# Second FFN of a diffusion layer: gated tiles turned by VectorE and DRAM, column blocks in pairs

## The chip, the core and the metric

The kernel runs on one core of one Trainium2 chip. The metric is the device time of one execution in microseconds; several executions are taken and their median is given. Everything is fp32, and the products that need fp32 accuracy are made from two halves: each operand is split into a rounded high part and the low rest, and three matmuls (high times high, low times high, high times low) stand for one product.

## The reference

The reference computes one layer of a diffusion backbone for 256 latent and 256 context tokens at width 2048: a half-step SwiGLU FFN, a mixing stage, a second half-step FFN for the latent tokens alone, and a final RMSNorm. The change lies in the second FFN, whose hidden width is 5632:

```python
def half_step_ffn(x, mod, i, g, w_up, w_down):
    h = adaln(x, g, mod, i)
    a, b = jnp.split(h @ w_up, 2, axis=-1)
    return x + 0.5 * mod[:, i + 2, None, :] * ((jax.nn.silu(a) * b) @ w_down)
```

## The kernel before

The hidden width of the second FFN is cut into eleven blocks of 512 columns (`FB` = 4 times 128), numbered 0 to 10. Block 0 is made in the order that the down projection needs. Blocks 1 to 9 (`QUADS`) go through `quad(n)`, which multiplies 2 x 2 quarters of the token matrix with quarters of the weights in seven products instead of eight: sums of token quarters (`n1`, `s4`, `s2`, `s3`) are made once, sums of weight quarters are made by loads that accumulate (`accum`, line 740, GpSimd's queue) into the tiles called `chain2` and `ra`, and two PSUM banks X and Y collect the products. Block 10 (`LAST`) goes through the plain `up`.

Each quad has seven products in order, each of two half-steps `q`: a11, a12, n1, s4, s2, s3, a22. Every half-step takes 128 x 2048 weights, which `split` (lines 128 and 129) turns into `hi` on ScalarE and `lo` on VectorE in two halves of 1024, and 12 matmuls. The `hi` and `lo` tiles have four buffers each, so the splits run at most two steps ahead of TensorE. A gated tile (128 tokens x 512 hidden columns) is silu(a) times b. Tile t = 0 of a block is finished by `c12`, after s2; tile t = 1 by `c21`, after a22.

The down projection needs the hidden columns on the partitions, so each gated tile has to be turned. `wait_turn(n, t, sa, sign)` puts the tile into the list `turn`; `turned()` (line 2044) is called after each step, and once `N_TURN` steps have passed and a slot of the three hidden blocks in flight (`N_HID`) is there, it makes four transposes on TensorE into a PSUM bank of the pool `tr` (line 2058), and splits the bank into `hid2h` on ScalarE (line 2061) and `hid2l` on VectorE (line 2063). `born` and `clock` count steps.

`down(n, n + 1)` is the down projection of two blocks: for each of four column blocks `cb` it takes two PSUM banks, multiplies block n and then block n + 1 into them, and adds the banks into `acc2`. Each of its steps is one load of weights (`load_split`, line 143, SyncE's queue, three `raw` buffers) and 24 matmuls.

`sequence()` weaves the two streams: "s" is a half-step of a quad, "u" a step of `up` or `down`. From the second quad on, a "u" stands after a12, n1, s2 and s3, so a quad is 14 half-steps and four steps. After the last step the rest of `turn` is emptied, and the down projection of blocks 8 and 9 and then that of block 10 follow. SyncE issues all loads of raw, the plain loads of `chain2` and `ra`, in one queue; a load that waits holds the ones behind it. The order of the instructions on an engine is made by a scheduler that goes by the order in the code and by when it takes an instruction's inputs to be ready.

The first FFN already turns the tiles of its blocks 1 to 10 in the way that the change brings to the second: `nc.vector.transpose` on VectorE (line 840), which turns each 32 x 32 square in its place, a store to DRAM (line 842), and four fetches for each quarter of a raw buffer that exchange the bands of 32 (line 711). There the blocks are fetched when their down projection begins.

Of the kernel before, what the change touches and what calls it, by code (L numbers as in the profile page):

```python
# [58 lines left out]
def tile_layer(ctx: ExitStack, tc: tile.TileContext, I: dict, out: bass.AP):  # L59
# [81 lines left out]
    def load_split(src, n=2048):  # L141
        raw = raw_tile(n)
        nc.sync.dma_start(raw, src)
        wt = split(raw, n)
        next(beside["load"], None)
        return wt
# [594 lines left out]
    with pool(name="f1u", bufs=1) as f1u:  # L741
# [91 lines left out]
        def turned():  # L833

            if not turn:
                return
            n, t, ca, spare = turn.pop(0)
            if (n, t) == (NB - 1, 3):
                spare = chp.tile([P, CB], F32, tag="stg", name="stg")
            pinned(nc.vector.transpose(spare, ca))  # L840
            s, tt = divmod(t, 2)
            nc.sync.dma_start(hidd[n][2 * tt + s], spare)
# [1088 lines left out]
    with f2x:  # L1931
        def hid_tiles():

            return [f2.tile([P, FB, T], F32R, tag=g, name=g, bufs=N_HID) for g in ("hid2h", "hid2l")]
# [106 lines left out]
        summed = set()  # L2041
        born, clock = {}, [0]

        def turned():

            if not turn:
                return
            n, t, sa, sign = turn[0]
            if clock[0] < born[n, t] + N_TURN:
                return  # L2050
            if n not in hids:
                if n - 1 not in hids or len(hids) - len(summed) >= N_HID:
                    return
                hids[n] = hid_tiles()
            turn.pop(0)
            tb = tbank()
            for j in range(FB):
                nc.tensor.transpose(tb[:, j * P : (j + 1) * P], sa[:, j * P : (j + 1) * P], ident)  # L2058
            t3 = tb.rearrange("p (j c) -> p j c", j=FB)
            hh, hl = (x[:, :, t * P : (t + 1) * P] for x in hids[n])  # L2060
            nc.scalar.activation(hh, t3, AF.Copy, scale=sign)
            if sign < 0:
                nc.vector.scalar_tensor_tensor(hl, t3, -1.0, hh.bitcast(F32), op0=ALU.mult, op1=ALU.subtract)
            else:
                nc.vector.tensor_tensor(hl, t3, hh.bitcast(F32), op=ALU.subtract)
            done.add((n, t))

        done = set()

        def wait_turn(n, t, sa, sign):  # L2070
            turn.append((n, t, sa, sign))
            born[n, t] = clock[0]
            turn.sort(key=lambda x: x[:2])

        def ca_tile():
            return f2b.tile([P, CB], F32, tag="ca", name="ca", bufs=3)

        def quad(n):

            add = lambda o, x, y: nc.vector.tensor_tensor(o, x, y, op=ALU.add)  # L2080
            mul = lambda o, x, y: nc.vector.tensor_tensor(o, x, y, op=ALU.mult)
            B, g = {}, {}

            def p1():
# [25 lines left out]
            def c21():  # L2110
                add(g["a"], B["Y"], g["a"])
                nc.scalar.activation(g["a"], g["a"], AF.Silu)
                mul(g["a"], g["a"], g["y"])
                wait_turn(n, 1, g["a"], -1.0)

            def chained(ab, c):
                return lambda q: accum(chain_[q], part(n, ab, c + q))
# [62 lines left out]
        def up(n):  # L2180

            sab = []
            for ab in range(2):
                bs = [bank() for _ in range(2)]
                for u in range(4):
                    wt = load_split(part(n, ab, u))
                    for j in range(4):
                        k = 4 * u + j
                        w = slice(j * CB, (j + 1) * CB)
                        for t in range(2):  # L2190
                            tt = slice(t * P, (t + 1) * P)
                            mm3(bs[t], h2hi[:, k, tt], h2lo[:, k, tt], *wt(w), k == 0, k == KT - 1)
                    if u == 3:
                        for t in range(2):
                            if ab:
                                nc.vector.tensor_tensor(sab[t], sab[t], bs[t], op=ALU.mult)
                                wait_turn(n, t, sab[t], 1.0)
# [14 lines left out]

        def down(*ns):

            for cb in range(NCB):
                c = slice(cb * CB, (cb + 1) * CB)
                bs = [bank() for _ in range(2)]
                for n in ns:
                    assert (n, 1) in done or not n
                    wt = load_split(I["w_dn2"][n, cb])  # L2220
                    for t in range(2):
                        block(bs[t], n, wt, t, n == ns[0], n == ns[-1])
                    if n == ns[-1]:
                        for t in range(2):
                            a = acc2[:, t, c]
                            if not ns[0]:
                                nc.scalar.activation(a, bs[t], AF.Copy)
                            else:
                                nc.vector.tensor_tensor(a, a, bs[t], op=ALU.add)
                            if n == LAST - 1:  # L2230
                                half_gated(a, a, late["g8"][:, c])
                                accum(a, x2d[t * P : (t + 1) * P, c])
                        if cb == NCB - 1:
                            summed.update(ns)
                    yield

        def units():
            yield from up(LAST)
# [37 lines left out]
        drain(down(LAST - 2, LAST - 1))  # L2276

        def last2():

# [69 lines left out]
def _laid_out(a):  # L2349
# [30 lines left out]
    for n in "12":  # L2380
        up, dn = a[f"w_ffn{n}_up"][0], a[f"w_ffn{n}_down"][0]
        nf = dn.shape[0] // P
        up = up.reshape(KT, P, 2, nf, P)

        rest = up[:, :, :, FB:].reshape(4, 4, P, 2, nf // FB - 1, CB)
        m[f"w_up{n}b"] = asc(rest.transpose(4, 3, 0, 2, 1, 5).reshape(nf // FB - 1, 2, 4, P, 2048))
        first = up[:, :, :, :FB].transpose(3, 2, 1, 0, 4).reshape(-1, 2, P, 2048)
        m[f"w_up{n}"] = asc(first[NPRE:])
        pre = first[:NPRE].reshape(2 * NPRE, P, KT, P)
        loads = []  # L2390
        for k0, k1 in BLOCKS if n == "1" else BLOCKS2:
# [3 lines left out]
        rows = dn.reshape(NF // FB, FB, P, NCB, CB).transpose(0, 3, 2, 1, 4).reshape(NF // FB, NCB, P, 2048)  # L2395
        if n == "1":
            turned = dn.reshape(NF // FB, 4, FB, 32, NCB, CB).transpose(0, 4, 1, 3, 2, 5).reshape(NF // FB, NCB, P, 2048)
            rows = np.concatenate([rows[:1], turned[1:]])
        m[f"w_dn{n}"] = asc(rows)
    w = a["w_in"][0]  # L2400

# [32 lines left out]
```

## Time and profile before

| What | Value |
| --- | --- |
| Median of 3 runs | 2591.18 us (2589.92 to 2593.5) |
| Profiled execution | 2588.91 us |
| its span | 2587.2 us |
| Granted TensorE clock, mean | 0.995 |
| Nine blocks of the second FFN | about 1950 to 2515 us of the span |

The profile is of one execution. Times in it are counted from the start of the span; what lies around the span is 1.7 us. An instruction of TensorE is shown with a modelled end, so the distance between two starts is what one takes when they follow each other closely. A wait is put down to what came last.

### The profile page before, as it was taken

What the parts mean: (1) busy time and instruction counts of PE and PEld (TensorE: products, weight loads), DVE (VectorE), ACT (ScalarE), POOL (GpSimd) and SP (SyncE); (2) the same over time, 40 slices, a digit from 0 to 9 for tenths busy, and PEclk for the clock granted to TensorE, in tenths of its full rate; (3) what the DMA queues carried; (4) which work ended last, traced back from release to release, by engine and by line L of the source; (5) the groups of instructions that cost most, each with busy time, mean ns of one, the idle gap of its engine ahead of it and who ended that gap; (6) DMA issues with size and microseconds to landing.
All of it is one profiled execution on the core that took longest, in us unless ns stands there. A gap on an engine that the chain in (4) does not pass through costs nothing. (4 is left out here: it accounts for less than half of the span.)

```text
span 2587.2 us, 33868 instructions
## 1 busy us (share of the span) xinstructions
PE 2555.3 (99%) x12486; PEld 2124.7 (82%) x12486; DVE 2206.6 (85%) x2924; ACT 1405.5 (54%) x1798; POOL 221.9 (9%) x271
## 2 busy tenths in 40 slices
PE   8999999999999999999999999999999999999998
PEld 5788888888887878888889889888898888888886
DVE  7789888888888788888887888898889888898987
ACT  5454444444444455444454347466486676667763
POOL 0000000100010100010110000120000000000001
PEclk8999999999999999999999999999999999999999
DMA  9989999999999999999987897776768999999985
GB/s 392 355 214 275 265 290 277 262 292 281 276 285 282 255 236 246 213 221 231 231 242 268 295 315 242 237 282 212 267 233 246 275 277 283 278 286 278 273 248 171
DMA packets 153478, 684.70 MB, mean 265 GB/s; under 512 B 22872, under 2 KB 43864, under 8 KB 92000
## 3 DMA queue, kind: packets, MB, share of 16 engines
q1 hardware_dynamic: 123936, 490.64, 51.7%
q0 software_dynamic: 29376, 191.90, 37.3%
q8 instruction: 98, 1.61, 0.2%
q14 instruction: 68, 0.56, 0.1%
HBM read 664.59 MB, written 17.89 MB: 264 GB/s over the span
## 5 line engine op out<-in xcount | busy, mean ns | idle before, releaser
L128 ACT ACTIVATE hi<-raw 128x1024 fp32r<-128x1024 f32 (+2 forms) x488 | 504.5, 1040 | 401.2 <-PE mm L152 298.7
L129 DVE TENSOR_TENSOR lo<-raw,hi 128x1024 fp32r<-128x1024 f32 (+2 forms) x476 | 567.2, 1204 | 105.7 <-ACT hi L128 87.4
L128 ACT ACTIVATE hi<-chain 128x1024 fp32r<-128x1024 f32 x352 | 370.1, 1059 | 352.6 <-PE mm L152 199.3
L129 DVE TENSOR_TENSOR lo<-chain,hi 128x1024 fp32r<-128x1024 f32 x352 | 425.2, 1219 | 92.5 <-ACT hi L128 81.2
L152 PE MATMUL mm<-hi,hhi 128*128 128x512 f32 (+3 forms) x1024 | 390.7, 382 | 0.0
L152 PE MATMUL mm<-lo,hhi 128*128 128x512 f32 (+3 forms) x1024 | 387.7, 379 | 1.9 <-DVE lo L129 1.8
L152 PE MATMUL mm<-hi,hlo 128*128 128x512 f32 (+3 forms) x1024 | 386.6, 378 | 0.0
L208 DVE SCALAR_TENSOR_TENSOR junk<-sraw,cBh 128x1024 fp8e5<-128x1024 f32 x192 | 234.3, 1220 | 40.5 <-DMA sraw<-in_w_mt 39.0
L152 PEld LDWEIGHTS mm<-lo,hhi 128*128 128x128 f32 x1024 | 192.8, 188 | 37.0 <-DVE lo L129 4.0
L152 PEld LDWEIGHTS mm<-hi,hlo 128*128 128x128 f32 x1024 | 193.0, 189 | 32.0
L152 PEld LDWEIGHTS mm<-hi,hhi 128*128 128x128 f32 x1024 | 192.9, 188 | 32.2 <-ACT hi L128 0.3
L129 DVE TENSOR_TENSOR lo<-ra,hi 128x1024 fp32r<-128x1024 f32 x104 | 126.2, 1222 | 25.6 <-ACT hi L128 21.7
L128 ACT ACTIVATE hi<-ra 128x1024 fp32r<-128x1024 f32 x104 | 110.1, 1062 | 64.0 <-PE mm L152 34.2
L152 PE MATMUL mm<-lo,hid2h 128*128 128x512 f32 x352 | 137.1, 389 | 0.0
L152 PE MATMUL mm<-hi,hid2h 128*128 128x512 f32 x352 | 137.1, 389 | 0.0
L152 PE MATMUL mm<-hi,hid2l 128*128 128x512 f32 x352 | 137.0, 389 | 0.0
L152 PE MATMUL mm<-hi,sumshl 128*128 128x512 f32 x400 | 123.2, 389 | 0.0
L208 DVE SCALAR_TENSOR_TENSOR sr<-sr,cBl 128x1024 f32<-128x1024 f32 x84 | 102.1, 1222 | 16.4 <-DMA sr<-in_w_mt 15.1
L740 POOL DMA_DIRECT2D chain<-in_w_up1b x60 | 53.1, 886 | 724.1 <-DVE lo L129 583.9
L152 PE MATMUL mm<-hi,sumshh 128*128 128x512 f32 x352 | 108.3, 389 | 0.0
L152 PE MATMUL mm<-hhi,hi 128*128 128x512 f32 (+1 forms) x288 | 101.4, 352 | 0.0
L152 PE MATMUL mm<-hhi,lo 128*128 128x512 f32 (+1 forms) x288 | 99.0, 344 | 0.0
(490 smaller groups left out, 5415.1 us busy)
## 6 DMA issues: line engine op xcount, KB each, us to landing
raw<-in_w_dn SPq DMA_DIRECT2D x70, 1024.0 KB, 10.0
chain<-in_w_up1b POOLq DMA_DIRECT2D x60, 1024.0 KB, 10.7
sraw<-in_w_mt SPq DMA_DIRECT2D x96, 512.0 KB, 8.4
sr<-in_w_mt SPq DMA_DIRECT2D x81, 512.0 KB, 5.7
raw<-in_w_up1b SPq DMA_DIRECT2D x40, 1024.0 KB, 9.1
mraw<-in_w_m SPq DMA_DIRECT2D x32, 1024.0 KB, 7.6
chain<-in_w_dn POOLq DMA_DIRECT2D x30, 1024.0 KB, 10.2
chain<-in_w_up2b POOLq DMA_DIRECT2D x28, 1024.0 KB, 11.4
```

Of the source, the lines that this page charges most:

```text
L128: scalar[0].activation(hi, src, AF.Copy)
L129: vector[0].tensor_tensor(lo, src, hi.bitcast(F32), op=ALU.subtract)
L152: tensor[0].matmul(out_ap, s, m, start=first and not n, stop=last and n == 2, skip_group_check=skip)
L208: ins = nc.vector.scalar_tensor_tensor(junk() if junk else raw, raw, 1.0, cB[s], op0=ALU.mult, op1=ALU.mult, accum_out=mT[:, i, s, kt, h : ...
L740: accum = lambda dst, src: nc.gpsimd.dma_start(dst, src, accum_op=ALU.add)
```

## The change

Tiles of blocks 1 to 9 are turned without TensorE. `c12` and `c21` multiply with a minus sign (`negative`) and hand a second tile, the one that held b, to `wait_turn` as `spare`. At the end of that step (`N_TURN` = 1, the count before was 2) `nc.vector.transpose` writes the tile into `spare`, turned in squares of 32. One step after that SyncE stores it to DRAM (`hid2d`); `N_STORE` = 3 steps after the turn, SyncE fetches it back into the first tile with four transfers, each of which puts one column band onto one band of 32 partitions in runs of 512 bytes; `N_MOVE` = 6 steps after the turn `halves` splits it into `hid2h` and `hid2l`, reading the four 32-wide runs of each group. The rows of the down weights of these blocks are laid out in the order that this gives. Block 10 still goes over TensorE, into a bank of the pool `mm`, which has six buffers; the pool `tr` is gone. The tiles `ca` have four buffers instead of three.

`down` takes two column blocks at a time: block n for both, then block n + 1 for both, in four banks. At the end its first two steps for blocks 8 and 9 run before the last gated tile is split.

```diff
-N_TURN = 2
+N_TURN = 1
+N_STORE = 3
+N_MOVE = 6
...
-        ps["mm"] = ctx.enter_context(pool(name="ps2", bufs=4, space=PSUM))
+        ps["mm"] = ctx.enter_context(pool(name="ps2", bufs=6, space=PSUM))
         psx = ctx.enter_context(pool(name="psx", bufs=1, space=PSUM))
-        ps["tr"] = ctx.enter_context(pool(name="pt2", bufs=2, space=PSUM))
...
+        hid2d = {n: dr.tile([2, P, CB], F32, name=f"hid2{n}") for n in QUADS}
+        moved = []
+        def halves(n, t, x, runs=False):
+            hh, hl = (y[:, :, t * P : (t + 1) * P] for y in hids[n])
+            if runs:
+                hh, hl = (y.rearrange("p j (a c) -> p a j c", c=32) for y in (hh, hl))
+            nc.scalar.activation(hh, x, AF.Copy)
+            nc.vector.tensor_tensor(hl, x, hh.bitcast(F32), op=ALU.subtract)
+            done.add((n, t))
...
-            for j in range(FB):
-                nc.tensor.transpose(tb[:, j * P : (j + 1) * P], sa[:, j * P : (j + 1) * P], ident)
-            t3 = tb.rearrange("p (j c) -> p j c", j=FB)
-            hh, hl = (x[:, :, t * P : (t + 1) * P] for x in hids[n])
-            nc.scalar.activation(hh, t3, AF.Copy, scale=sign)
-            if sign < 0:
-                nc.vector.scalar_tensor_tensor(hl, t3, -1.0, hh.bitcast(F32), op0=ALU.mult, op1=ALU.subtract)
...
+            if spare is not None:
+                turn.pop(0)
+                nc.vector.transpose(spare, sa)
+                moved.append((clock[0], n, t, sa, spare))
+            elif room(n):
+                turn.pop(0)
+                tb = bank()
+                for j in range(FB):
+                    nc.tensor.transpose(tb[:, j * P : (j + 1) * P], sa[:, j * P : (j + 1) * P], ident)
+                halves(n, t, tb.rearrange("p (j c) -> p j c", j=FB))
+        def stored(n, t, sa, spare):
+            nc.sync.dma_start(hid2d[n][t], spare)
+        def fetched(n, t, sa, spare):
+            rows = hid2d[n][t].rearrange("(a r) (b x) -> b r a x", a=4, b=4)
+            for b in range(4):
+                nc.sync.dma_start(sa[32 * b : 32 * b + 32].rearrange("r (a x) -> r a x", a=4), rows[b])
+        def arrived():
+            for then, *x in moved:
+                if clock[0] == then + 1:
+                    stored(*x)
+                elif clock[0] == then + N_STORE:
+                    fetched(*x)
+            if moved and clock[0] >= moved[0][0] + N_MOVE and room(moved[0][1]):
+                _, n, t, sa, _ = moved.pop(0)
+                halves(n, t, sa.rearrange("p (a j c) -> p a j c", a=4, j=FB), True)
...
-            return f2b.tile([P, CB], F32, tag="ca", name="ca", bufs=3)
+            return f2b.tile([P, CB], F32, tag="ca", name="ca", bufs=4)
...
-                mul(g["a"], g["a"], g["b"])
-                wait_turn(n, 0, g["a"], -1.0)
+                negative(g["a"], g["b"])
+                wait_turn(n, 0, g["a"], g["b"])
...
-            for cb in range(NCB):
-                c = slice(cb * CB, (cb + 1) * CB)
-                bs = [bank() for _ in range(2)]
+            for c0 in (0, 2):
+                bs = {}
                 for n in ns:
+                    for cb in (c0, c0 + 1):
...
             clock[0] += 1
+            arrived()
             turned()
...
-        while turn:
-            clock[0] += 1
-            turned()
-        before_final()
-        drain(down(LAST - 2, LAST - 1))
+        before_final()
+        final = down(LAST - 2, LAST - 1)
+        for gap in (1, N_STORE - 1):
+            clock[0] += gap
+            arrived()
+            next(final)
+        while moved:
+            clock[0] += N_MOVE
+            arrived()
+        while turn:
+            turned()
+        drain(final)
```

More of the change, by code (lines that the diff above doesn't have):

```diff
@@ L2047, in turned @@
                 return
-            n, t, sa, sign = turn[0]
+            n, t, sa, spare = turn[0]
             if clock[0] < born[n, t] + N_TURN:
                 return
[L2051 to L2056, printed above, removed]
-            for j in range(FB):
-                nc.tensor.transpose(tb[:, j * P : (j + 1) * P], sa[:, j * P : (j + 1) * P], ident)
@@ L2068, in tile_layer, with wait_turn @@
         done = set()
-        def wait_turn(n, t, sa, sign):
-            turn.append((n, t, sa, sign))
+        def wait_turn(n, t, sa, spare):
+            turn.append((n, t, sa, spare))
             born[n, t] = clock[0]
@@ L2112, in c21 @@
                 nc.scalar.activation(g["a"], g["a"], AF.Silu)
-                mul(g["a"], g["a"], g["y"])
-                wait_turn(n, 1, g["a"], -1.0)
+                negative(g["a"], g["y"])
+                wait_turn(n, 1, g["a"], g["y"])
             def chained(ab, c):
@@ L2213, in down @@
         def down(*ns):
-            for cb in range(NCB):
-                c = slice(cb * CB, (cb + 1) * CB)
-                bs = [bank() for _ in range(2)]
+            for c0 in (0, 2):
+                bs = {}
                 for n in ns:
[L2219 to L2223, printed above, removed]
-                        for t in range(2):
[L2225 to L2235, printed above, removed]
+                    for cb in (c0, c0 + 1):
+                        assert (n, 1) in done or not n
+                        c = slice(cb * CB, (cb + 1) * CB)
+                        if n == ns[0]:
+                            bs[cb] = [bank() for _ in range(2)]
+                        wt = load_split(I["w_dn2"][n, cb])
+                        for t in range(2):
+                            block(bs[cb][t], n, wt, t, n == ns[0], n == ns[-1])
+                        if n == ns[-1]:
+                            for t in range(2):
+                                a = acc2[:, t, c]
+                                if not ns[0]:
+                                    nc.scalar.activation(a, bs[cb][t], AF.Copy)
+                                else:
+                                    nc.vector.tensor_tensor(a, a, bs[cb][t], op=ALU.add)
+                                if n == LAST - 1:
+                                    half_gated(a, a, late["g8"][:, c])
+                                    accum(a, x2d[t * P : (t + 1) * P, c])
+                            if cb == NCB - 1:
+                                summed.update(ns)
+                        yield
         def units():
@@ L2395, in _laid_out @@
         rows = dn.reshape(NF // FB, FB, P, NCB, CB).transpose(0, 3, 2, 1, 4).reshape(NF // FB, NCB, P, 2048)
+        turned = dn.reshape(NF // FB, 4, FB, 32, NCB, CB).transpose(0, 4, 1, 3, 2, 5).reshape(NF // FB, NCB, P, 2048)
         if n == "1":
-            turned = dn.reshape(NF // FB, 4, FB, 32, NCB, CB).transpose(0, 4, 1, 3, 2, 5).reshape(NF // FB, NCB, P, 2048)
             rows = np.concatenate([rows[:1], turned[1:]])
+        else:
+            rows = np.concatenate([rows[:1], turned[1:-1], rows[-1:]])
         m[f"w_dn{n}"] = asc(rows)
```

13 lines of the change are left out of this document (8 added, 5 removed).

## The prediction

> **What bounds the kernel now.** I read the page's busy times first, then the table by stage for the stretch in which the nine blocks run, then TensorE's timeline at one of the groups of transposes that go.
>
> ```profile
> span 2587.2 us, 33868 instructions
> PE 2555.3 (99%) x12486; PEld 2124.7 (82%) x12486; DVE 2206.6 (85%) x2924; ACT 1405.5 (54%) x1798; POOL 221.9 (9%) x271
> ...
> core 0: us, PE busy (x) PEld busy (x) DVE busy (x) ACT busy (x) POOL busy (x), PEclk, DMA share, GB/s
> 2000.00:2500.00 500.00, 499.46 (x2232) 412.21 (x2231) 438.35 (x416) 347.15 (x367) 41.89 (x48) 1.00 0.94 275
> ```
>
> In these 500 us TensorE is busy for 499.46, at the full granted clock, so a stall of another engine costs nothing until TensorE waits for it, and an instruction taken from TensorE is time gained. A block of the nine is 14 half-steps of 12 matmuls, four steps of 24 and 8 transposes: 272 of the 2232 instructions, or 60.9 us. The same row gives a second number almost as full: the DMA engines are at 0.94.
>
> ```profile
> q0 software_dynamic: 7312, 53.35, 52.8%
> q1 hardware_dynamic: 11849, 86.19, 41.5%
> ...
> ACT hi L128 <- DMA chain<-in_w_up2b: 18.1, 7, 3.9
> ```
>
> These are the two queues over 1990 to 2500 us: the accumulating loads that GpSimd issues (q0) take the larger share, SyncE's plain loads (q1) the rest. The third line, of the waits, says that ScalarE already waits for an accumulated chain, up to 3.9 us, once in nearly every block.
>
> **What the change takes away.** 18 groups of four transposes on TensorE.
>
> ```profile
> 2000.12 0.39 PE L152 MATMUL mm<-lo,h2hi 128*128 128x512 f32 x1
> 2000.35 0.60 PE L2058 MATMUL tr<-ident,ca 128*128 128x128 f32 x4
> 2000.70 0.71 PE L152 MATMUL X<-hi,s3f 128*128 128x512 f32 x2
> 2001.26 0.40 PE L152 MATMUL X<-lo,s3f 128*128 128x512 f32 x1
> ...
> L2058 PE MATMUL tr<-ident,ca x72: 270/272/304, 2000.3 to 2514.6; 128*128 128x128 f32 x72
> ```
>
> The starts count, since durations overlap. A matmul's pitch is 2000.35 - 2000.12 = 0.23 us. From the first transpose to 2001.26 lie four transposes and two matmuls: 0.91 - 0.46 = 0.45 us for the group. 72 transposes are 18 groups: 8.1 us off TensorE, the whole of the gain, and a block falls from 60.9 to 60.0 us.
>
> **What it puts on VectorE and ScalarE.**
>
> ```profile
> L840 DVE STREAM_TRANSPOSE c<-ca x20: 691/704/711, 208.3 to 922.5; 128x512 f32<-128x512 f32 x20
> ...
> L2063 DVE SCALAR_TENSOR_TENSOR hid2l<-tr,hid2h x18: 683/684/694, 2002.6 to 2515.5; 128x512 fp32r<-128x512 f32 x18
> ...
> L2061 ACT ACTIVATE hid2h<-tr x20: 578/585/602, 2001.3 to 2515.4; 128x512 fp32r<-128x512 f32 x20
> ```
>
> The first FFN turns tiles of this shape on VectorE in 0.704 us (line 840): 18 x 0.704 = 12.7 us. VectorE is idle for 61.7 us of the 500 and takes them there; without that cover they would be 12.7 us. The sign moves from the low half (0.684 us) into the product, both 128x512, so neither side changes. The split into halves reads SBUF in place of PSUM; I keep 0.585 and 0.684 us. The pairs of column blocks in the down projection have the same matmuls and weights in another order, and the six banks hold what four and two held: nothing on the path while the next block's tiles are there, which the last tile below decides.
>
> **What it puts on the DMA rings.** 18 stores and 72 fetches. A store of 0.262 MB at q1's rate (86.19 MB in 41.5% of 510 us) is 0.64 us of all engines. The fetches move runs of 512 B. In the first FFN there is a stretch, 1004 to 1008 us, where nothing else moves:
>
> ```profile
> q1 hardware_dynamic: 1861, 0.93, 122.8%
> ```
>
> 0.93 MB in 4 us: 0.262 MB are 1.13 us. Two tiles per block add 3.5 us. The rings need 0.94 x 60.9 = 57.2 us per block now and 60.7 after, against 60.0 of TensorE. So the slack of the rings is gone. The bound of this is from 0 (the share was not all necessary time) to 0.7 us per block.
>
> **The wait that it adds.** Before, a tile went through PSUM in under 2 us. Now the split on ScalarE stands behind a store and a fetch that itself waits on SyncE for the store to land. Queued behind the split on ScalarE are the weight splits of the next steps, and TensorE waits for those; behind the fetch on SyncE are the next raw, ra and chain loads. The price is the round trip against the time to the split's place in ScalarE's order.
>
> ```profile
> 2185.44 0.68 DVE L2081 TENSOR_TENSOR ca<-ca 128x512 f32<-128x512 f32 x1
> 2202.55 3.49 DVE L129 TENSOR_TENSOR lo<-chain,hi 128x1024 fp32r<-128x1024 f32 x3
> 2208.82 0.69 DVE L2081 TENSOR_TENSOR ca<-ca,cy 128x512 f32<-128x512 f32 x1
> ...
> 2198.58 2.15 ACT L128 ACTIVATE hi<-ra 128x1024 fp32r<-128x1024 f32 x2 [2.22 <-DMA ra<-in_w_up2b]
> 2201.01 1.06 ACT L128 ACTIVATE hi<-chain 128x1024 fp32r<-128x1024 f32 x1 [0.29 <-PE Y L152]
> ...
> 2216.48 1.06 ACT L128 ACTIVATE hi<-chain 128x1024 fp32r<-128x1024 f32 x1 [0.30 <-PE Y L152]
> 2218.07 0.63 ACT L2090 ACTIVATE ca<-ca 128x512 f32<-128x512 f32 x1 [0.54 <-DVE ca L2080]
> 2222.41 2.01 ACT L128 ACTIVATE hi<-chain 128x1024 fp32r<-128x1024 f32 x2 [3.70 <-DMA chain<-in_w_up2b]
> ...
> 2205.07 0.39 PE L152 MATMUL X<-hi,h2hi 128*128 128x512 f32 x1
> ...
> 2227.17 0.50 PE L152 MATMUL Y<-lo,n1f 128*128 128x512 f32 x1 [0.53 <-DVE lo L129]
> ```
>
> Tile 0 of this block: product done at 2186.1, turned at 2186.8. Six steps later by the kernel's clock is after the last split of the block (hi<-ra, done 2200.7) and before that of the next block's first step (2201.01): 14.2 us from 2186.8. Tile 1: turned at 2210.2; six steps later is after the first half of n1's split (2216.48) and the silu (2218.07), before the second half at 2222.41: 12.2 us.
>
> ```profile
> L842 SPq DMA_DIRECT2D hid<-c x20: 326/327/1792, 209.1 to 923.2; - x20
> ...
> DMA to landing us min/median/max: 3.7/7.6/12.5
> ...
> L711 SPq DMA_DIRECT2D hidh<-hid x20: 325/480/704, 949.0 to 1229.8; - x20
> ...
> DMA to landing us min/median/max: 3.2/7.2/28.8
> ```
>
> Line 842 stores such tiles, line 711 fetches with the same exchange of bands; both stand in a stretch whose rings are as full. Ends: 3.7 + 3.2 and 12.5 + 28.8 us. I take the medians, as the rings here are no emptier, and three more issues before the last of four fetches, 3 x 0.48: 7.6 + 1.4 + 7.2 = 16.2 us, and 0.58 for the split's own activation.
>
> Tile 0: 16.8 - 14.2 = 2.6 us late on ScalarE. The low half of that next split ends by 2203.8 (the first of three from 2202.55) where TensorE wants it by about 2205.3: 1.5 us of cover, so 1.1 us of stall, 9 times: 9.9 us. Tile 1: 16.8 - 12.2 = 4.6 us, with no cover (TensorE waits there already, 0.53 us at 2227.17), 8 times: 36.8 us. Together 46.7 us. But a block that is 5 us longer leaves the rings 5 us more, and round trips shorten; between all of it and none I take half, 23.4 us.
>
> SyncE's held loads I cost at nothing:
>
> ```profile
> 2193.79 0.33 SPq L143 DMA_DIRECT2D raw<-in_w_dn  x1
> ...
> DMA to landing us min/median/max: 5.4/10.6/12.0
> ...
> 2212.46 1.05 ACT L128 ACTIVATE hi<-raw 128x1024 fp32r<-128x1024 f32 x1
> ```
>
> The raw block issued at 2193.79 lands by 2204.4 (median of line 143) and is split at 2212.46, three buffers later: 8.1 us of cover against a hold of at most a store's landing, 7.6. Without that cover it would be up to 7.6 us a block.
>
> The last tile 1:
>
> ```profile
> 2513.41 0.68 DVE L2081 TENSOR_TENSOR ca<-ca,cy 128x512 f32<-128x512 f32 x1
> ...
> 2510.62 0.19 PEld L152 LDWEIGHTS mm<-hi,hid2h 128*128 128x128 f32 x1
> ```
>
> Turned at 2514.8; with 8.3 to 16.2 us of round trip (minimum and median, with the issues) and 1.3 of halves its block could start between 2524.4 and 2532.3. TensorE has two steps of block 8 (48 matmuls, 10.9 us), 12 matmuls of tile 0 (2.7) and the group for the last block (0.9). Its weight load at 2510.62 opens the two steps, so it gets there at about 2525: 0 to 7 us; few loads are left, so I take 1.
>
> Sum: -8.1 + 23.4 + 1 = +16.3 us, on a profiled execution of 2588.91 us: 2605.2. That execution was 2.3 us under the median of 2591.18, so 2607.5 on the scale of the runs. What a measurement of this kernel can tell from no change is about 0.2%, 5.2 us.
>
> **The rivals.** *All hidden, faster.* If the two landings and the issues take under 12 us together, no split is late, and the 8.1 us stay: 2583 to 2586. For it: the minima add up to 8.3 us; and in the first FFN TensorE stays full with the same stores at a DMA share of 0.99:
>
> ```profile
> 600.00:680.00 80.00, 80.00 (x355) 66.07 (x354) 70.37 (x96) 36.97 (x42) 7.05 (x8) 1.00 0.99 279
> ```
>
> Against it: there the fetch comes tens of microseconds after the store, here after two steps. 0.28. The Trainium skill, "DMA: Bandwidth & Descriptors", section "Anatomy of one DMA", fits a transfer as 2.0 us plus bytes over 436 GB/s: an estimate of 2.6 us for a store, by which this rival would win. The median of 7.6 us says that a full ring is not that case.
>
> *The rings become the bound, no change.* No split is late, but the rings need 60.7 us a block where TensorE needs 60.0: nine blocks of 60.7 instead of 60.9 are 2 us less, and the last tile gives 1 to 4 back: 2588 to 2595. For it: the sum above. Against it: it needs every other wait hidden. 0.12.
>
> *The fetch starves, much slower.* Where q0 has a backlog, the rings alternate packet by packet, so a fetch of 32 small packets per engine waits for 32 large accumulating ones. The first FFN shows it, 885 to 901 us:
>
> ```profile
> q0 software_dynamic: 445, 3.25, 97.6%
> q1 hardware_dynamic: 445, 0.23, 6.9%
> ```
>
> One for one, and such a fetch landed after up to 28.8 us. Tile 1's fetch falls where q0 holds two accumulating loads. If all of it does, ScalarE waits 20 us more there, and even half of that in five of the blocks is 50 us: 2640 to 2680. Against it: the two loads are gone after some 14 us. 0.15. The Trainium skill (same page, "Queues, rings and completion order") has an engine drain a packet of about 9 to 17 descriptors before it turns to another ring; by that the fetch would pass in three or four turns and this rival would fall. The equal counts in the rows speak against that here.
>
> **How the numbers follow.** Forecast, ScalarE late, 2597 to 2640: 0.45. Faster by over 0.2% is the first rival, 0.28; within 0.2% the second, 0.12; slower by over 0.2% the forecast and the third, 0.60. The forecast's own range is 2597 (a quarter of the stalls) to 2639 (all of them: 2607.5 + 23.4 + up to 8 at the end). The range that holds 8 in 10 goes from the first rival's 2583 to 2645, and leaves out most of the third.
>
> **What would show it.** Right: ScalarE's halves of the nine blocks show an idle time before them that ends on a DMA into ca, TensorE waits for hi or lo two to four microseconds later, and its share in this stretch falls below 97%. The group of 72 transposes is gone and eight remain. Wrong: the halves wait for nothing, blocks of 60.0 us. If blocks grow although the halves don't wait, SyncE's held loads or the rings are the cause, and raw or ra loads end the waits. If store and fetch land in under 9 us together, the round trip was the mis-sized term.

## The result and the profile after

The changed kernel takes 2660.95 us (2659.37 to 2662.84) against 2591.1 us of the kernel before in the same comparison: a ratio of 1.0268, 95% interval 1.0255 to 1.0281. That is 70 us slower where 16 were forecast, and above the range. The changed kernel's lines are numbered a little higher: 132 and 133 are the splits, 156 the matmuls, 2062 and 2063 the halves, 2075 VectorE's turn, 2085 the store, 2090 the fetch.

The stretch from 2000 to 2500 us, as quoted for before (same columns):

```profile
2000.00:2500.00 500.00, 460.31 (x1914) 368.63 (x1913) 394.66 (x381) 299.74 (x324) 36.56 (x42) 0.96 0.90 258
```

TensorE was busy for 499.46 us of these 500 and is now busy for 460.31; its granted clock fell from 1.00 to 0.96. A block, counted from the first matmul of a11 to that of the next a11, took 60.9 us before. The following two rows of TensorE's timeline are such a pair, 67.8 us apart; the mean of the last seven periods is 68.9.

```profile
2169.80 0.63 PE L156 MATMUL X<-hi,h2hi 128*128 128x512 f32 x1
...
2237.61 0.40 PE L156 MATMUL X<-hi,h2hi 128*128 128x512 f32 x1
```

So 8 us in each of the later blocks, 60 us in the stage, are lost where the change is; 6.8 us more are lost after the last a11. What is waited for (total us, times, longest), 1960 to 2590 us:

```profile
ACT hid2h L2062 <- DMA ca<-hid: 80.6, 17, 7.3
...
DVE hid2l L2063 <- ACT hid2h L2062: 59.1, 17, 5.7
...
PEld Y L156 <- ACT hi L132: 35.1, 15, 4.4
PE Y L156 <- ACT hi L132: 28.8, 14, 4.0
PEld Y L156 <- DVE lo L133: 25.1, 27, 4.0
```

ScalarE stands at the halves until the fetch has landed, VectorE stands behind it at the low half, and TensorE then waits for `hi` and `lo` of the products behind. One round trip on SyncE, ScalarE, VectorE and TensorE, and last the row of the stretch from 2194 to 2197 us (columns as above):

```profile
2176.21 0.33 SPq L147 DMA_DIRECT2D raw<-in_w_dn  x1
2176.83 0.33 SPq L2085 DMA_DIRECT2D hid<-cy  x1
2179.08 0.33 SPq L147 DMA_DIRECT2D raw<-in_w_dn  x1
2188.17 2.04 SPq L2090 DMA_DIRECT2D ca<-hid  x4
2190.30 0.38 SPq L147 DMA_DIRECT2D raw<-in_w_dn  x1
...
2192.11 0.63 ACT L2062 ACTIVATE hid2h<-ca 128x512 fp32r<-128x512 f32 x1 [3.43 <-DMA ca<-hid]
...
2192.77 0.69 DVE L2063 TENSOR_TENSOR hid2l<-ca,hid2h 128x512 fp32r<-128x512 f32 x1 [2.52 <-ACT hid2h L2062]
...
2190.51 0.61 PE L156 MATMUL Y<-hi,n1f 128*128 128x512 f32 x2
2194.65 0.79 PE L156 MATMUL Y<-lo,n1f 128*128 128x512 f32 x1 [3.53 <-DVE lo L133]
...
2196.10 0.63 PE L156 MATMUL Y<-lo,n1f 128*128 128x512 f32 x1
2196.52 0.63 PE L156 MATMUL mm<-hi,hid2h 128*128 128x512 f32 x1
2196.95 0.63 PE L156 MATMUL mm<-hi,hid2l 128*128 128x512 f32 x1
...
2198.44 0.39 PE L156 MATMUL mm<-hi,hid2h 128*128 128x512 f32 x1
2198.67 0.39 PE L156 MATMUL mm<-hi,hid2l 128*128 128x512 f32 x1
...
2194.00:2197.00 3.00, 2.35 (x6) 1.87 (x7) 3.00 (x4) 2.19 (x3) 0.00 (x0) 0.54 0.18 71
```

The store is issued at 2176.83, the fetch that needs it only at 2188.17, and nothing behind it on SyncE moves meanwhile: the next raw load goes at 2190.30. The halves run at 2192.11, TensorE stalls for 3.5 us, and afterwards its matmuls start 0.42 us apart for some three microseconds, before they are back at 0.23. In that stretch the granted clock is 0.54, and the DMA engines, to which SyncE gave nothing from 2179 to 2188 us, are at 0.18. Intervals between matmul starts at this half speed are 66 in 1960 to 2510 us (0.2 us more each: 13 us); the kernel before has none there.

### The profile page after: what moved, and what is told of

Read it like the earlier page. It is cut to its first block, busy times and chain, and to the rows that moved or that the text cites. A ratio compares the mean times of both kernels' runs of the same rounds, so it can differ in the third digit from the quotient of the medians.

```text
span 2658.5 us, 33926 instructions
## 1 busy us (share of the span) xinstructions
PE 2575.7 (97%) x12414; PEld 2126.4 (80%) x12414; DVE 2215.4 (83%) x2942; ACT 1398.4 (53%) x1798; POOL 220.9 (8%) x271
## 6 DMA issues: line engine op xcount, KB each, us to landing
chain<-in_w_up2b POOLq DMA_DIRECT2D x28, 1024.0 KB, 10.4
```

## Experiments

Before took 2591 to 2593 us in all comparisons. Two pairs have the same order of instructions on SyncE and TensorE in this stage, and on ScalarE and VectorE but for a few halves: e1 and e5, and the changed kernel and e16. They differ by 7 and 6 us, so smaller differences are not read. The table has the median, the ratio to before, the mean of the last seven periods of a11, and of 2030 to 2450 us the granted clock and the DMA share.

| Kernel | Median us | Ratio (95%) | Block us | Clock | DMA |
| --- | --- | --- | --- | --- | --- |
| before | 2591 | 1 | 60.9 | 1.00 | 0.94 |
| changed | 2661 | 1.0255-1.0281 | 68.9 | 0.96 | 0.90 |
| e1 halves late, kept | 2620 | 1.0095-1.0134 | 65.1 | 0.98 | 0.95 |
| e2 no store, no fetch | 2593 | 0.9992-1.0011 | 61.1 | 1.00 | 0.94 |
| e3 trip beside | 2627 | 1.0120-1.0150 | 64.8 | 1.00 | 0.94 |
| e4 pairs alone | 2599 | 1.0009-1.0031 | 61.3 | 1.00 | 0.94 |
| e5 as e1 | 2628 | 1.0091-1.0155 | 64.9 | 0.99 | 0.95 |
| e6 beside, old tile | 2615 | 1.0060-1.0108 | 63.4 | 1.00 | 0.96 |
| e7 e2, single columns | 2590 | 0.9984-1.0009 | 60.9 | 1.00 | 0.94 |
| e11 e7, 0.5 MB less | 2590 | 0.9976-1.0003 | 60.7 | 1.00 | 0.92 |
| e13 e3 + ScalarE's wait | 2648 | 1.0195-1.0226 | 67.4 | 0.96 | 0.92 |
| e14 e3 + VectorE's wait | 2655 | 1.0223-1.0260 | 68.2 | 0.96 | 0.91 |
| e15 e3 + both waits | 2656 | 1.0211-1.0257 | 68.0 | 0.96 | 0.92 |
| e16 eight steps, not kept | 2655 | 1.0221-1.0256 | 68.0 | 0.97 | 0.91 |
| e17 six steps, kept | 2649 | 1.0205-1.0267 | 68.2 | 0.96 | 0.92 |
| e18 e1, tile 0 fetched later | 2604 | 1.0033-1.0060 | 62.0 | 1.00 | 0.98 |

**e1, the halves late.**

```diff
-N_MOVE = 6
+N_MOVE = 10
...
-            nc.scalar.activation(hh, x, AF.Copy)
-            nc.vector.tensor_tensor(hl, x, hh.bitcast(F32), op=ALU.subtract)
+            hold = tc.keep_in_program_order if runs else (lambda i: i)
+            hold(nc.scalar.activation(hh, x, AF.Copy))
+            hold(nc.vector.tensor_tensor(hl, x, hh.bitcast(F32), op=ALU.subtract))
```

> The changed kernel with the halves of the turned tiles asked for ten steps after the turn in place of six, and kept at that place in ScalarE's and VectorE's order. Theory A (ScalarE's splits stand behind halves that wait for store and fetch, and every TensorE stall of some 2 us is paid again by 3.4 us at half the clock): the 84 us of idle time before the halves go under 10, no half-clock stretch is left between 1960 and 2510 us, blocks of 60.0 to 60.9 us, 2584 to 2595 us in all. Rival B (the rings and SyncE's loads held behind store and fetch are what is late): splits still wait, now for raw and ra loads, blocks of 65 us and more, 2630 to 2660 us. Rival C (the pairwise down projection with its common pool of banks): 2650 to 2660 us.

2620 us, between the theories: no wait of the halves for the fetch is left, and 33 to 41 us (with e5, below) went with it, but blocks of 65 us remain, and 40 intervals at half speed.

**e2, no trip.** `stored` and `fetched` are not called; the halves read `spare`.

> The changed kernel without the store and the fetch: the halves read the tile as VectorE turned it, so its bands are not exchanged. Theory A and rival B alike: the stalls go, 8.1 us of transposes stay off TensorE: blocks of 60.0 us, 2581 to 2587 us. Rival C (pairs and banks): hardly less than the changed kernel, over 2640 us. What is under 2591 us here is all that the change could bring.

A miss for all: 2593 us. Without any trip the change is worth nothing.

**e3, the trip beside.**

```diff
-            if spare is not None:
+            if spare is not None and room(n):
                 turn.pop(0)
                 nc.vector.transpose(spare, sa)
                 moved.append((clock[0], n, t, sa, spare))
-            elif room(n):
+                tb = bank()
+                for j in range(FB):
+                    nc.tensor.transpose(tb[:, j * P : (j + 1) * P], sa[:, j * P : (j + 1) * P], ident)
+                halves(n, t, tb.rearrange("p (j c) -> p j c", j=FB))
+            elif spare is None and room(n):
...
-                _, n, t, sa, _ = moved.pop(0)
-                halves(n, t, sa.rearrange("p (a j c) -> p a j c", a=4, j=FB), True)
+                moved.pop(0)
```

> The changed kernel with VectorE's turn, the store and the fetch made as before, but their result unused: TensorE transposes the tiles again and the halves read its bank. Only the rings, SyncE and VectorE carry the trip; no instruction of ScalarE waits for it. Theory A: no stalls, the transposes are back (8.1 us): 2588 to 2598 us. Rival B (rings and held loads): the stalls stay, with raw and ra loads late, 2630 us and more. Rival C: 2640 us and more.

2627 us: 28 us over the pairs alone (e4, below), with no instruction of ScalarE waiting for the trip. That is far above A's range and just under B's: rival B lives, beside A.

**e4, the pairs.** `down` as changed, one pool of six banks, transposes as before.

> The kernel before with one part of the change: the down projection takes column blocks in pairs, and six banks serve matmuls and transposes from one pool. Theory A and rival B: no change, 2588 to 2596 us. Rival C (the pairs hold four banks for longer, or the last blocks are put in a worse order): 2620 us and more; a small part of it, 2597 to 2605 us, would show as a longer end after 2515 us.

2599 us: 2 to 8 us more than before, 0.3 us a block and 3.3 us after the last a11 (141.1 us against 137.8). Rival C is out as the main cause; the small part of it that was named is there.

**e5, the fetch asked for later.** e1 with `N_STORE = 6` and the fetches kept in order.

> As the first of these kernels (halves asked for ten steps after the turn and kept there), and the four fetches asked for six steps after the turn in place of three, kept there in SyncE's order, so that SyncE's next loads do not stand behind a fetch that waits for its store. Theory R (rings: at a DMA share of about 0.94 they give no more in this stage, and the trip's bytes lengthen every block): nothing but SyncE's waits change, blocks of 64.5 to 65.5 us, 2614 to 2624 us. Theory H (SyncE's loads held behind the fetch, 175 us in the nine blocks of the first of these kernels, are what comes late): SyncE's waits for hid go under 40 us, blocks of 61 to 62 us, 2592 to 2602 us.

2628 us, but it says nothing of H: in these blocks SyncE's order came out as in e1, with one load between store and fetch. It stands as a second e1.

**e6, SyncE not held.** In e3, the fetch reads a tile that landed long ago:

```diff
-            rows = hid2d[n][t].rearrange("(a r) (b x) -> b r a x", a=4, b=4)
+            rows = hid2d[max(n - 1, min(hid2d))][t].rearrange("(a r) (b x) -> b r a x", a=4, b=4)
```

> As the kernel with the trip beside (TensorE transposes the tiles, the trip's result is unused), but the fetch reads the tile that the block before stored, which landed long ago: the same bytes in the same packets at the same place of SyncE's order, and SyncE waits for no store. Theory R: as there, blocks of 64 to 65.5 us, 2619 to 2630 us. Theory H: blocks of 61 to 62 us, 2595 to 2604 us.

2615 us, below theory R's range and far above H's: 12 us under e3, 16 over e4. The first is what the hold was worth there, but not cleanly: without the dependence, the scheduler put the fetch of tile 1 directly behind the store, where e3 has a load between. The second is the same bytes and issues, and VectorE's turn, without the hold.

**e7, no trip and single column blocks.** e2 with the `down` and the two pools of before.

> As the kernel without store and fetch (halves read VectorE's own tile, bands not exchanged), with the down projection of the kernel before: column blocks one by one, four banks for it and two for transposes. Theory R: the rings already set blocks of 61 us with nothing added (57.4 us of ring time at a share of 0.94), so the 8.1 us are not won here either: 2587 to 2593 us. Rival P (the pairs took them): blocks of 60.0 us, 2580 to 2586 us.

2590 us. The pairs did not eat the gain. Its first two full blocks took 59.8 and 60.3 us, as the prediction's 60.0; the later ones 60.9 to 62.1.

**e8, e9, e10 and e12, ScalarE held.** e8 and e12 repeat tile 1's first half in the kernel before. e9 and e10 put 26 small copies into e3 where the halves stood, without and with store and fetch:

```diff
+                for _ in range(N_HELD):
+                    tc.keep_in_program_order(nc.scalar.activation(scratch, ident[:, :64], AF.Copy))
```

> The kernel before, with ScalarE's first half of tile 1 made 1, 2, 3 ... 9 times over in the nine blocks, the same result each time (0.585 us each, 36 more in all: 21.1 us on ScalarE), so that TensorE stalls by a little more in each block. Clock theory: from a stall of about 2 us on, matmuls right after it run at 0.43 us in place of 0.227 for 3.4 us, and the block pays 1.3 to 1.7 us beyond its stall: five or six such stretches, 2610 to 2621 us. Rival: the clock does not follow a stall (what was seen was the load of that moment): no half-speed stretch, 2603 to 2612 us.

> The kernel with the trip beside, without its store and fetch, and with ScalarE held for as long as the changed kernel's halves wait (84 us in 18 waits: 4.65 us each) at the place where these halves stood: 26 copies of 128x64 elements, some 0.18 us each, whose result is unused. Theory A (the wait of the halves alone stalls TensorE, nearly one for one, and the clock adds to it): 2640 to 2665 us. Theory I (such a hold is covered by the lead that the splits have, and costs only where the trip has eaten that lead): 2597 to 2612 us.

> The same hold of ScalarE, with store and fetch made beside it and unused. Theory A: the trip's 34 us and the hold's 45 to 70 us add up, 2670 to 2700 us. Theory I: 2650 to 2670 us, as the changed kernel (2661 us), though the hold alone costs under 20 us. If it stays at 2625 to 2640 us, the halves' waits are a sign and no cause, and the changed kernel loses its last 40 us in another way.

> The kernel before, with ScalarE's first half of tile 1 made 5, 6, 7 ... 13 times over in the nine blocks, now kept together in ScalarE's order: 4 to 12 more of 0.585 us, holds of 2.3 to 7.0 us. Clock theory: the first blocks are covered (under 2 us of stall, no half speed), the last four or five stall by 2 us and more, and after each the matmuls run at 0.43 us in place of 0.227 for about 3.4 us: 2603 to 2618 us. Rival (no such tie): stalls of the same size, no matmul at 0.43 us, 2597 to 2610 us.

2594.6 (e8), 2606.8 (e9), 2632.0 (e10) and 2594.3 us (e12). By the ranges, e9 fits theory I, and e10 would make the halves' waits a sign and no cause. Neither follows, and none of the four tells the theories apart, since the copies did not stay together. ScalarE's timeline of e10:

```profile
2180.31 0.53 ACT L2109 ACTIVATE scratch<-ident 128x64 f32<-128x64 f32 x2
2180.74 1.04 ACT L134 ACTIVATE hi<-ra 128x1024 fp32r<-128x1024 f32 x1
2181.69 0.53 ACT L2109 ACTIVATE scratch<-ident 128x64 f32<-128x64 f32 x2
2182.12 1.04 ACT L134 ACTIVATE hi<-raw 128x1024 fp32r<-128x1024 f32 x1
```

Keeping instructions in order keeps it among those that are kept; splits slip between. What they show is another thing: ScalarE has the time. More work than the changed kernel's 84 us of waiting (468 copies of 0.26 us), spread between the splits, costs 5 us (e10 over e3, within the scatter) to 8 us (e9 over e4).

**e11, 0.5 MB less a block.**

```diff
-        nc.sync.dma_start(raw, src)
+        nc.sync.dma_start(raw[:, : n // 2] if half else raw, src[:, : n // 2] if half else src)
```

> The kernel without store and fetch and with single column blocks, with 0.5 MB less to load a block of some 16.7 MB: of the second column block's down weights of the nine blocks only the first half is loaded and split, and stands for the other half too (one split of 1.05 us less on ScalarE). Theory R (57.4 us of ring time at a share of 0.94 set the 61 us): 55.7 us of ring time now, so TensorE's 60.0 us set the block and the 8.1 us appear at last: 2578 to 2586 us. If the rings are not the bound: unchanged, 2587 to 2593 us.

2590 us, blocks of 60.7: theory R falls. Fewer bytes do not bring the 8.1 us.

**e13, e14 and e15, one wait.** In e3, where the halves of the changed kernel stand in the engine's order, one small instruction that reads the fetched tile:

```diff
+                nc.scalar.activation(scratch[:, :32], sa[:, :32], AF.Copy)                            # e13, e15
+                nc.vector.tensor_tensor(scratch[:, 32:], sa[:, :32], sa[:, 32:64], op=ALU.add)         # e14, e15
```

> The kernel with the trip beside (TensorE transposes the tiles; 2627 us), and where the halves of the changed kernel stand in ScalarE's order, one copy of 128x32 elements of the fetched tile into a spare tile: ScalarE waits for the trip as in the changed kernel, and no other work depends on it. Theory A (one wait up to a fixed landing makes every split behind it late, however far ahead ScalarE was, and TensorE stalls): 2650 to 2668 us, ScalarE idle some 60 to 90 us before these copies. Theory S (that wait is a sign of late loads only): 2624 to 2636 us, and the 40 us come from the halves as such, which TensorE's down projection waits for.

> The same with the wait on VectorE instead: one addition of 128x32 elements of the fetched tile, where the low halves of the changed kernel stand. Theory A with ScalarE as the engine that matters: less than with ScalarE's wait, 2627 to 2645 us. If VectorE's wait is what counts (the low parts of the splits and the combinations behind it): 2650 to 2668 us, and ScalarE's wait alone is near 2630 us. Theory S: 2624 to 2636 us.

> Both waits, as the changed kernel has them. Theory A: 2652 to 2670 us, no more than a few us over the larger of the two alone, since both end with the same landing. Theory S: 2624 to 2636 us.

2648, 2655 and 2656 us: 21, 28 and 29 us over e3; e13 lies just under theory A's range. A wait that carries next to no work makes the loss, on either engine, and both waits together cost no more than one. The waits of e13, and of e14:

```profile
ACT scratch L2106 <- DMA ca<-hid: 53.8, 14, 6.8
```

```profile
DVE scratch L2106 <- DMA ca<-hid: 38.8, 12, 7.0
...
PEld Y L156 <- DVE lo L133: 27.5, 15, 4.2
```

Theory A holds, in a wider form than I gave it: I had expected VectorE's wait to cost less than ScalarE's. Both make one half of every split.

**e16 and e17, the place.** The changed kernel with `N_MOVE = 8`, and with `N_MOVE = 6` and the halves kept in order.

> The changed kernel with the halves asked for eight steps after the turn in place of six, nothing kept in order: some 5 us later, about as long as they waited. Theory A: most of their 84 us of idle time goes, and with it most of the 40 us: 2618 to 2640 us, the rest being what store and fetch cost beside. Theory S: 2650 us and more.

> The changed kernel with the halves kept at the place where its steps ask for them (six after the turn): on ScalarE three splits and a silu later than now for tile 0, one split later for tile 1; between the changed kernel (2661 us, waits of 84 us) and the one with halves kept ten steps after the turn (2620 to 2628 us, no waits). Theory A (the place of the wait decides): the waits fall to 30 to 60 us and the time lies between, 2630 to 2650 us. Theory S (the place does not matter): 2655 to 2661 us.

e16, 2655 us, fits theory S's numbers and yet is no evidence for it: the halves stand at the same places in ScalarE's order as in the changed kernel, and wait as they did. The step in the code does not set the place; the scheduler does, by when it takes the fetch to have landed. e17, 2649 us, at the edge of A's range, moved them: 51 us of waits (7 of them, up to 8.7) in 1960 to 2520 us, one stall a block in place of two, but a longer one, as in this row, with 0.79 us for a matmul behind it:

```profile
2251.64 1.22 PE L156 MATMUL Y<-hi,n1f 128*128 128x512 f32 x2 [4.33 <-ACT hi L132]
2252.89 0.79 PE L156 MATMUL Y<-lo,n1f 128*128 128x512 f32 x1
```

Its blocks are no shorter (68.2 us), so the loss does not go down in proportion to the waits.

**e18, the fetch behind more loads.** e1 with `N_STORE = 8` and the fetches kept; only tile 0's moved, behind four loads in all but the first of these blocks (three were expected). The last block's tile 0 goes without its four fetches, which fall out at the end of the stage.

> The halves kept ten steps after the turn, and the fetch asked for eight steps after it and kept: for tile 0 it now stands three loads behind its store in SyncE's order (one load before), for tile 1 as before. Theory H (SyncE's held loads carry part of the remaining 27 us): SyncE's wait for tile 0's store, 73 us in the nine blocks, goes under 20 us, and the time falls by 4 to 10 us, to 2612 to 2619 us. Theory R alone (only the bytes count): 2619 to 2628 us as with the fetch behind one load.

2604 us, 16 to 24 under e1 and e5, more than theory H's range. SyncE's waits, e1 and then e18:

```profile
SPq L2091 <- DMA hid<-cy: 101.9, 8, 15.9
SPq L2091 <- DMA hid<-ca: 72.9, 8, 10.5
```

```profile
SPq L2091 <- DMA hid<-cy: 86.5, 8, 12.1
```

The hold for tile 0 (`ca`) is gone and the blocks fell from 65 to 62.0 us. ScalarE's waits for the accumulated weights fell with it, from 65.2 us in e1 to 32.4 (`chain` and `ra` together). In exchange the halves of tile 0 wait again for their later fetch:

```profile
ACT hid2h L2063 <- DMA ca<-hid: 13.7, 6, 2.7
```

The windows row of e18 shows what the DMA engines then do:

```profile
2030.00:2450.00 420.00, 410.34 (x1788) 333.89 (x1788) 369.91 (x360) 282.66 (x306) 36.62 (x42) 1.00 0.98 284
```

A share of 0.98 against 0.95 in e1. A fetch that holds SyncE leaves the rings short of loads, and with the hold gone the share rises and the blocks shorten.

## Why the prediction was wrong

**What held.** The sign and the mechanism: the halves' idle time ends on a DMA into `ca` (80.6 us for 17 of the 18 in the rows above), TensorE waits for `hi` or `lo` right behind, and its share in the stretch is 92%, below the 97% named. The group of 72 transposes is gone and eight remain. VectorE's turns took 0.71 us each, as put. The round trip had nearly the right length with its parts wrong; stores and fetches in the changed kernel:

```profile
L2085 SPq DMA_DIRECT2D hid<-cy x9: 326/327/327, 2030.3 to 2586.3; - x9
...
DMA to landing us min/median/max: 4.7/10.4/14.3
...
L2090 SPq DMA_DIRECT2D ca<-hid x72: 325/424/1500, 2017.5 to 2592.4; - x72
...
DMA to landing us min/median/max: 1.8/3.1/5.8
```

10.4 + 1.4 + 3.1 = 14.9 us against 16.2. The store goes out right behind a load (2176.21 and 2176.83 above); the fetch finds little ahead of it, since SyncE has issued nothing for 9 us (2179.08 to 2188.17 above; in e18, where loads went out ahead of it, four fetches issued from 2215 us on took 16 to 18 us). The starving rival thus fell for a reason that it did not name. The estimate of 2.6 us for a store by the Trainium skill ("DMA: Bandwidth & Descriptors", section "Anatomy of one DMA", whose fit is for transfers that GpSimd issues, while these stores are SyncE's) was met by none here: the shortest took 4.7 us. One sum was off without effect: a quarter of the stalls gives 2595.8 us, where the lower end of the range says 2597.

**The step that failed first: the halving of the wait.** 46.7 us were worked out and half was taken, 23.4, since longer blocks would empty the rings. The runs show 33 to 41 us (changed against e1 and e5), and 21 to 29 us in e13 to e15, where the rest of e3 is there already. With emptier rings the trip was in fact shorter: at a DMA share of 0.90 a store took 10.4 us (median), where it took 14.6 in e1 at 0.95 and 14.0 in e3 at 0.94. But the halving set out from the 7.6 us of the first FFN, and so counted a saving from a trip that was shorter than any of these. Two things more were missing from that working. VectorE stands still too, 59 us behind the high half, and e14 shows that a wait of VectorE alone is enough. And the stalls bring half-speed matmuls, 13 us of the changed kernel's loss by the count above, of which e1 keeps 8 and e5 4: a term that the sum did not have. I had also put tile 0's halves a split too late and tile 1's too early in ScalarE's order, since I read the places from the steps in the code; e16 shows that they don't follow the steps.

**The step that failed second: SyncE's held loads at nothing.** The cover that I showed, 8.1 us for a raw load, was true of that load and not of the others behind the fetch. The changed kernel's own waits of SyncE, 1960 to 2520 us:

```profile
SPq L2090 <- DMA hid<-ca: 69.5, 8, 10.3
...
SPq L2090 <- DMA hid<-cy: 59.4, 7, 9.2
...
SPq L2085 <- DVE cy L2075: 32.6, 7, 7.1
```

Two holds of 8 to 9 us in each block, not one of at most 7.6. Removing one of the two gave 16 to 24 us (e18); e6 gave 12 for both where nothing else waited. The cost of one, some 2 to 3 us a block, lies within the prediction's own bound without the cover, 7.6 us a block. The third row is a hold that the prediction did not have at all: SyncE stands at tile 1's store until VectorE has turned the tile, because in most blocks the scheduler put that store ahead of a raw load that goes first in e1. In e1, e13 and e14 this wait is 5 us in all, so a part of the 33 to 41 us above may be this hold; no run takes it away alone.

**The last tile.** From the last a11 to the end it is 144.6 us against 137.8: 6.8 more, about what one of the longer blocks costs; 3.3 of it stand in e4 too, which has the pairs alone. The 1 us put for the last tile can't be told apart from that.

**The gain that did not come.** With everything of the trip taken away, 8.1 us fewer on TensorE are worth 0 (e2) to about 2 us (e7), within the scatter. Not the pairs (e7) and not the bytes (e11) keep them. In e7 ScalarE waits longer for the accumulated weights than in the kernel before, here first, in the same stretch:

```profile
ACT hi L128 <- DMA chain<-in_w_up2b: 20.6, 8, 3.9
ACT hi L128 <- DMA ra<-in_w_up2b: 11.5, 5, 2.8
```

```profile
ACT hi L132 <- DMA chain<-in_w_up2b: 23.9, 12, 3.8
...
ACT hi L132 <- DMA ra<-in_w_up2b: 23.4, 10, 3.9
```

The profile's chain, which follows the last instruction back to what released each step, shows where the time goes. From 2000 to 2515 us of the kernel before it stays on TensorE (first row: 99.6%); in e7 it leaves TensorE in four of the blocks, in this way:

```profile
by line: PE mm L152 36.7%; PE Y L152 34.6%; PE X L152 26.5%; PE tr L2058 1.8%; DVE lo L129 0.2%; issue 0.2%; DVEq L129 0.0%
```

```profile
2126.49 1.15 DVE lo L133
...
2127.65 14.75 DMA ra<-in_w_up2b
...
2142.47 5.88 issue
...
2151.22 14.11 DMA ra<-in_w_up2b
...
2166.53 1.24 DVE lo L133
```

VectorE's split releases the buffer, SyncE's plain load fills it in 14.75 us, GpSimd's accumulating load goes out 8.8 us later and lands after 14.11 us, and the next split follows: 37.7 us from release to landing. The same legs stand in the chains of e2 and e11; fewer bytes leave them as long. So this trip of the weights sets the block at 60.7 to 61 us as soon as TensorE does not. No run shortens it, so this is read from the chains and not tested; VectorE's turns, which e2, e7 and e11 also have, do not stand in them. In e1, too, the chain runs over such legs, and there the accumulating load takes 16.3 to 18.1 us, against 13.1 to 14.1 in e7. That TensorE was busy for 499.46 of 500 us did not mean that the next limit was far away.

**The rings.** 60.7 us a block were reckoned with the trip; 0.98 x 62.0 = 60.8 us are what e18 moves. That term was right. Whether the rival built on it would come true if nothing were held up, no run here shows.

**The account of the 70 us:** the halves' waits with the clock, and with what SyncE's stand at tile 1's store adds, 33 to 41; SyncE's hold for tile 0, 16 to 24; the remaining 12 (e18 against before) are tile 1's hold, which was not taken away on its own, the halves' waits that e18 still has, the bytes, and the pairs. These pieces are not independent: e6, nearly without a hold, is 16 us over e4, more than those 12. The profiles, one execution each, allow a second count, from the first a11 of block 1 to the end; that leaves out what runs before it and sets the start of this stage anywhere from 1946 to 1961 us. By it the changed kernel is 67 us over before, e1 36, e5 34 and e18 10: 31 to 33 us for the first piece and 25 to 26 for the second. No version beat the kernel before, and none is in sight: the one without any trip only equals it.

## What to carry to other kernels

A wait on a transfer, in an engine that works in order, costs not that engine's time but the lead of all that stands behind it: more than 84 us of small work between the splits cost 5 to 8 us, one wait per tile 21 to 29. Before a path is put through DRAM, write down for each of the queues it crosses, the issuing one first, what stands behind the waiting instruction, and give the dependent transfer and its reader so much distance that neither waits. And before time is taken off a full engine, look for what is next behind it, a full queue or a long round trip: here it was at most 0.2 us a block away (60.9 against 60.7).

## What the runs showed of the hardware

Short stalls cost twice. After gaps of TensorE of 2 to 4 us (up to 6.5 in e17), and some of 1.2 to 1.8, the matmuls started 0.42 us apart in place of 0.23, mostly for about 3 us, then recovered. It is the granted clock: it reads 0.50 from 2194.2 to 2197.6 us of the changed kernel and 1.00 in the 3.4 us on either side. It does not follow every gap: in e5 three gaps of 2.7 us had nothing behind them. The counts in 1960 to 2510 us are 66 such intervals in the changed kernel, 63 to 70 in e13 to e16, 52 in e17, 40 in e1, 19 in e5 and at most one in before, e3 and e18. No run takes the half speed away and leaves the same stalls, so what it costs by itself is a count and not a test. The Trainium skill, "TensorE: Matmul & The Clock Gate", section "Why this matters for your kernels", has the clock fall for idle gaps of more than about 3 us; the traces show it for gaps of about 2 us as well (e1: 2.1 us at 2429 us).

The DMA engines, which looked full at 0.94 in the kernel before, reached 0.98 in the same stage with the trip's bytes added and the issuing queue held less than in e1 (e18).
